# Front of a hybrid decoder block in another order, its row scale on GpSimd, and two work tiles lent to weight loads

## The chip, the cores and the metric

The kernel runs on one core of a Trainium2 chip. The metric is the device time of one execution in microseconds (us). Before the change, three runs gave 628.66, 625.45 and 625.47 us: a median of 625.47 us. The engines are named as the profile names them: PE is TensorE's matmul and PEld its weight load, DVE is VectorE, ACT is ScalarE, POOL is GpSimd, SP is SyncE, whose queue only issues DMAs here.

## What is computed

One decoder layer on 256 tokens of 1024 channels, float32 in and out:

```
h = rms_norm(x, attn_norm_w)
z = h @ w_in                      # keys, values, queries, branches, gates
y_ret = retention(...)            # 4 heads, chunks of 128
y_sc  = sb * causal_dwconv(sc * sx, sc_conv_w)
y_nsa = nsa_attention(...)        # compressed + selected + window branch
merged = g_ret*(y_ret@w_ret_out) + g_sc*(y_sc@w_sc_out) + g_nsa*(y_nsa@w_nsa_out)
x = x + merged @ w_mix_out
x = x + conv_glu_ffn(rms_norm(x, ffn_norm_w), w_up, conv_w, w_down)
return rms_norm(x, final_norm_w)
```

The compressed branch of the sparse attention takes overlapping blocks of 32 keys (and values), adds a position table, and passes each block through `gelu(blk @ w1) @ w2`. With 256 tokens all four selectable key blocks of 64 are selected, so the selected branch is causal attention over all keys.

## The kernel before, in words

**Pieces.** All weights come as pieces of 128 x 2048 float32 (1 MB), in two halves of 128 x 1024. A half is loaded into a tile `raw` by SP's queue (L129), then split in two numbers whose sum is the weight: ACT casts it to the high part `whi` (L136), DVE subtracts to get the low part `wlo` (L137). A product is three matmuls (`mm3`, L163): high x high, high x low, low x high. A piece is an `Item` with `load`, `split` and `consume`. `raw` has four buffers, so two pieces; the split parts have five pairs of buffers and, in the front, a sixth (`w_m`, in the room of a later tile): three pieces. A half's `raw` buffer is free again once DVE has its `wlo`.

**The order of the pieces.** `stream` (L175) walks a list of items: in step i it emits the loads of item i+2 (`la=2`), the split of item i+1 (`ls=1`), then the matmuls of item i and what takes their result out of PSUM (its `evac`), then what `later` had put off by one item, then `pull` steps of the generator `attention`. That is program order. Every engine runs its own instructions in one order that is fixed when the program is built; the framework keeps data dependences but may place an instruction ahead of others that stand before it in the program. `tc.keep_in_program_order` forbids it for one instruction. The result shows in the trace: the copies of the position table (L349), written long after the first value pieces, ran on ACT at 13.67 and 15.00 us.

**PSUM.** Eight banks: three in turn with the tag `mm`, five with the tag `aux`. A feature-major piece (`f_consume`, L193: keys, queries, short-convolution pieces) takes one `mm` bank; a token-major pair of pieces (`t_pair`, L210: the gates) takes two and keeps them over both pieces. A bank is free again when its evac is done.

**The front** (the first list of items): five `vv` items (values and branch gates, on x that is not yet normalized, `xw`), then `kc` and `vc` (compressed keys and values, also on `xw`, scaled by the row scale on the way out, L338), then `ks` and `kw` (selected and window keys) and everything else on the normalized `hT`. The order is: vv, kc, vc, ks, kw, gate 0, w1 0, query 0, gate 1, w1 1, gate 2, w1 2, gate 3, w1 3; and in a second list, which also pulls the attention: query 1, x0, x1, x4, b0, x2, x3, ... (x and b are the short convolution's pieces, `scx` and `sbp`).

**The row scale.** ACT squares x (L278), POOL adds the squares up (L279, L281), PE sums over partitions, DVE and POOL make `rs0` (L285, L286), DVE and PE spread it over partitions, and DVE copies it to `rstd` (L295). `head_rest` with all this stands behind the fourth vv item. `head_h` (L306) then makes `hT`: eight DVE multiplications of x by norm weight and `rstd` (L308), four ACT casts (L311), four DVE subtractions (L312). Its first half stands ahead of kc's matmuls, its second ahead of vc's. x is in the tile with the tag `ysch`, the squares in the tile with the tag `yscl`; both rooms are taken later by the short convolution's result.

**The evacs of the front.** `cmp_raw_evac` (L331) scales kc or vc into `dd` and copies it, shifted by a token, to the other 64 partitions by a DMA on ACT's queue; one item later `cmp_blocks` (L344) clears `bb` on POOL, puts the position table in (L349, L350) and splits `dd` into it (ACT L355, DVE L356). `w1_consume` multiplies `bb` with the w1 pieces. `key_evac` (L359) takes ks or kw to `kdh` and `kdl` by four ACT copies (L370) and four DVE subtractions (L371) in turn, then copies each half to the other partitions with DMAs on POOL's queue (L374). `q_evac` does the same for queries without a DMA.

**The attention** (`attention`, L648) gives 36 steps, pulled between the 23 items of the second list: scores, softmax on DVE and ACT, transposes, products with the values.

Of the kernel before, what the change touches and what calls it, by code (L numbers as in the profile page):

```python
# [63 lines left out]
def kernel(  # L64
# [55 lines left out]

    class Item:
# [4 lines left out]
        def load(self):  # L126
            for ap, n in self.srcs:
                r = wpool.tile([128, 1024], F32, tag="raw", name="raw", bufs=RAWB)
                nc.sync.dma_start(r[:, :n], ap)  # L129
                self.raw.append(r)  # L130

# [43 lines left out]
    def stream(items, gen=None, la=2, ls=1):  # L175
        n = len(items)
        for i in range(-la, n):
            if 0 <= i + la < n and not items[i + la].raw:
                items[i + la].load()
            if 0 <= i + ls < n and not items[i + ls].parts:  # L180
                items[i + ls].split()
            if i < 0:
                continue
            due = pending[:]
            pending.clear()
            items[i].consume(items[i].parts)
# [76 lines left out]
    def attw(k):  # L263
        return attn_w[:, k : k + 1]
# [34 lines left out]
    def head_rstd():  # L299
        ps = bank("aux")  # L300
        for t in range(2):
            mm(ps[:, t : t + 1], sq[:, 0, t * 128 : (t + 1) * 128], ones[:, 0:1], True, True)
        row_rstd(ps[:, 0:2], rs0)
        spread(rs0, sq[:, 1, :], rstd)

    def head_h(half):  # L306
        for k in range(4 * half, 4 * half + 4):
            V.scalar_tensor_tensor(xT_s[:, k, :], xT_s[:, k, :], attw(k), rstd, op0=OP.mult, op1=OP.mult)  # L308
            if k % 2 == 1:
                c = slice(k - 1, k + 1)  # L310
                A.copy(hT[0][:, c, :], xT_s[:, c, :])  # L311
                V.tensor_sub(hT[1][:, c, :], xT_s[:, c, :], f32(hT[0][:, c, :]))  # L312
# [18 lines left out]
    def cmp_raw_evac(kv):  # L331
        def evac(ps):
            p4 = ps.rearrange("p (b t) -> p b t", b=2)
            d = cp.tile([128, 4, S], F32, tag="dd", name="dd", bufs=2)
            dv = d.rearrange("p (b two) t -> p b two t", two=2)
            for par in range(2):
                r = slice(par * 64, par * 64 + 64)
                V.tensor_tensor(dv[0:64, :, par, :], p4[r], rstd[r].unsqueeze(1).to_broadcast([64, 2, S]), op=OP.mult)  # L338
            nc.scalar.dma_start(d[64:128, :, 0 : S - 1], d[0:64, :, 1:S])
            later(lambda: cmp_blocks(kv, d))  # L340

        return evac

    def cmp_blocks(kv, d):  # L344
# [4 lines left out]
        A.copy(bb[:, :, 0, 0, 15], pos)  # L349
        V.tensor_sub(bb[:, :, 1, 0, 15], pos, f32(bb[:, :, 0, 0, 15]))  # L350
        d5 = d.rearrange("p g (c l two) -> p l g c two", two=2, l=8)
        for i in range(2):
            src = d5[:, :, :, i : i + 15, 0]
            hi, lo = (bb[:, 8 * i : 8 * i + 8, x, :, 0:15] for x in range(2))
            A.copy(hi, src)  # L355
            V.tensor_sub(lo, src, f32(hi))  # L356
        blk[kv] = bb.rearrange("p l s g c -> p l (s g c)")

    def key_evac(name):  # L359
        def evac(ps):  # L360
            p4 = ps.rearrange("p (b t) -> p b t", b=2)
            for par in range(2):
                r = slice(par * 64, par * 64 + 64)
                o = slice(64 - par * 64, 128 - par * 64)
                kv4 = [k.rearrange("p (b two) t -> p b two t", two=2) for k in kd]
                for t in range(2):
                    c = KCOL[(name, t)]
                    src = p4[r, :, t * 128 : (t + 1) * 128]
                    dst = [k[r, :, par, c : c + 128] for k in kv4]
                    A.copy(dst[0], src)  # L370
                    V.tensor_sub(dst[1], src, f32(dst[0]))  # L371
# [109 lines left out]
    def vv_items():  # L481
        st = {}

        def go(ks, off):
            def run(parts):
# [3 lines left out]
                for k in ks:  # L489
                    hi, lo = parts[k - off]  # L490
                    for t in range(2):
# [9 lines left out]
                        )  # L501
                if ks[-1] == 7:
# [266 lines left out]
    def proj(n, **kw):  # L769
# [41 lines left out]
    stream(items)  # L811
# [9 lines left out]
    p_sc, g_nsa = proj("o_sc"), gate("o_nsa")
    made = {"x": scx, "b": sbp, "q": nqp, "s": lambda j: p_sc[j], "n": lambda j: g_nsa[j]}
    for n, e in enumerate(plan):
        items.append(made[e[0]](int(e[1])))
        items[-1].pull = (36 * (n + 1)) // len(plan) - 36 * n // len(plan)
    stream(items, att)
# [443 lines left out]
```

## Time and profile before

| | |
|---|---|
| median of three runs | 625.47 us |
| the profiled execution, its own time | 626.15 us |
| span of its profile | 624.3 us |
| busy: PE, DVE, ACT, POOL | 603.4, 477.6, 387.1, 21.2 us |
| matmuls | 3948 |
| granted TensorE clock, mean | 0.994 |
| moved by DMA | 111.82 MB |

A profile page holds one execution. Times are in us, "mean ns" in nanoseconds. The table of windows gives, for a stretch of the span, each engine's busy time with its instructions (xN), the granted TensorE clock (PEclk, 1.00 is full speed), the busy share of the DMA engines and the GB/s moved. In the timeline each row has start, duration, engine, line, operation, tile written and tiles read, and at its end, in brackets, the idle time of the engine before it and what ended it. A matmul's duration in the timeline is longer than the distance to the next one, since they are pipelined; the distance is what counts. In the table of waits a row has the waiting engine, what it waited for, the total, the times and the longest.

### The profile page before, as it was taken

The numbers are of one execution on the slowest core, as the hardware profiler recorded it, in microseconds if no ns is written. First come the engines' busy times: TensorE is split into PE (matmuls) and PEld (weight loads), VectorE is DVE, ScalarE is ACT, GpSimd is POOL, SyncE is SP. The second block draws the span as 40 slices with busy tenths as digits, with TensorE's granted clock in tenths as the row PEclk, the third lists the DMA queues.
The fourth block names the chain that finished last, engine by engine and source line by source line (L and its number), as shares of the span: only waits on it lengthen the run. The fifth ranks groups of instructions, "written<-read, shape, count | busy, mean of one in ns | idle before, by whom it ended". The sixth has DMA issues, their size and how long they took to land.

```text
span 624.3 us, 10611 instructions
## 1 busy us (share of the span) xinstructions
PE 603.4 (97%) x3948; PEld 548.2 (88%) x3948; DVE 477.6 (76%) x935; ACT 387.1 (62%) x752; POOL 21.2 (3%) x32
## 2 busy tenths in 40 slices
PE   8986999999999999999999999999999999999994
PEld 8975989999999888898888888888999999999993
DVE  6897568998989887679657977568898777777754
ACT  7665667798988887644554565446756555555532
POOL 5102000000000000000000100000000000000001
PEclk9999999999999999999999999999999999999998
DMA  7759876444354344465655477675347755566401
GB/s 257 246 174 254 236 248 221 140 162 139 108 164 136 122 147 136 136 219 171 215 193 165 132 252 247 202 265 174 109 153 254 234 178 181 186 201 202 138 1 67
DMA packets 32995, 111.82 MB, mean 179 GB/s; under 512 B 3632, under 2 KB 5552, under 8 KB 32816
## 3 DMA queue, kind: packets, MB, share of 16 engines
q1 hardware_dynamic: 30240, 106.00, 52.3%
q10 hardware_dynamic: 1552, 4.09, 2.1%
q0 software_dynamic: 1152, 1.05, 1.2%
q8 instruction: 31, 0.51, 0.3%
q14 instruction: 20, 0.16, 0.1%
HBM read 108.51 MB, written 1.05 MB: 175 GB/s over the span
## 4 chain that ended last, share of the span: by engine, by line
PE 76%; DVE 7%; ACT 7%; DMA 6%; issue 2%; POOL 1%; SPq 0%; POOLq 0%; ACTq 0%; DVEq 0%
PE ps_mm L161 56%; PE ps_aux L161 17%; DMA raw<-in_wp_dram 5%; DVE wlo L137 3%; ACT whi L136 2%; PE ps_aux L598 1%; ACT P L575 1%; DMA xT_s<-in_xT_dram 1%; DVE qs L533 0%; POOL sq L281 0%; PE ps_aux L627 0%; DVE hTl L312 0%; DVE dd L338 0%; DVE xT_s L308 0%; ACT low L641 0%
## 5 line engine op out<-in xcount | busy, mean ns | idle before, releaser
L137 DVE TENSOR_TENSOR wlo<-raw,whi 128x1024 fp32r<-128x1024 f32 (+1 forms) x197 | 237.7, 1210 | 85.8 <-ACT whi L136 84.1
L136 ACT CAST whi<-raw 128x1024 fp32r<-128x1024 f32 (+1 forms) x197 | 203.0, 1035 | 132.3 <-PE ps_mm L161 82.2
L161 PE MATMUL ps_mm<-hTh,whi 128*128 128x256 f32 x352 | 99.4, 282 | 6.2 <-DVE kdl L371 5.2
L161 PE MATMUL ps_mm<-h,whi 128*128 128x256 f32 x576 | 102.2, 281 | 0.0
L161 PE MATMUL ps_mm<-hTh,wlo 128*128 128x256 f32 x352 | 99.0, 281 | 0.5 <-DVE wlo L137 0.5
L161 PE MATMUL ps_mm<-hTl,whi 128*128 128x256 f32 x352 | 98.8, 281 | 0.6 <-DVE hTl L312 0.6
L161 PEld LDWEIGHTS ps_mm<-h,whi 128*128 128x128 f32 x576 | 88.5, 188 | 0.7
L161 PE MATMUL ps_mm<-h,wlo 128*128 128x256 f32 x288 | 80.9, 281 | 0.0
L161 PEld LDWEIGHTS ps_mm<-hTh,whi 128*128 128x128 f32 x352 | 67.1, 191 | 6.9 <-issue 5.3
L161 PEld LDWEIGHTS ps_mm<-hTl,whi 128*128 128x128 f32 x352 | 67.1, 191 | 1.3 <-DVE hTl L312 1.0
L161 PEld LDWEIGHTS ps_mm<-hTh,wlo 128*128 128x128 f32 x352 | 67.0, 190 | 0.9 <-DVE wlo L137 0.9
L161 PE MATMUL ps_mm<-whi,hTh 128*128 128x512 f32 x152 | 59.7, 393 | 0.0
L161 PE MATMUL ps_mm<-whi,hTl 128*128 128x512 f32 x152 | 59.3, 390 | 0.0
L161 PE MATMUL ps_mm<-wlo,hTh 128*128 128x512 f32 x152 | 59.3, 390 | 0.0
L161 PEld LDWEIGHTS ps_mm<-h,wlo 128*128 128x128 f32 x288 | 55.3, 192 | 0.0
L575 ACT ACTIVATE P<-P,st 128x16 f32<-128x16 f32 (+2 forms) x96 | 37.9, 397 | 0.8 <-DVE st L570 0.7
L161 PE MATMUL ps_aux<-whi,acth 128*128 128x512 f32 x88 | 34.2, 389 | 0.0
L161 PE MATMUL ps_aux<-wlo,acth 128*128 128x512 f32 x88 | 34.2, 389 | 0.0
L161 PE MATMUL ps_aux<-whi,actl 128*128 128x512 f32 x88 | 34.2, 389 | 0.0
L161 PEld LDWEIGHTS ps_mm<-whi,hTl 128*128 128x128 f32 x152 | 28.5, 188 | 6.1
L161 PEld LDWEIGHTS ps_mm<-whi,hTh 128*128 128x128 f32 x152 | 28.6, 188 | 5.6
L161 PEld LDWEIGHTS ps_mm<-wlo,hTh 128*128 128x128 f32 x152 | 28.6, 188 | 5.5
(250 smaller groups left out, 1141.2 us busy)
## 6 DMA issues: line engine op xcount, KB each, us to landing
raw<-in_wp_dram SPq DMA_DIRECT2D x194, 512.0 KB, 4.4
raw<-in_wv_dram SPq DMA_DIRECT2D x8, 280.0 KB, 3.9
x2b<-in_xt_dram ACTq DMA_DIRECT2D x1, 1024.0 KB, 4.7
xT_s<-in_xT_dram SPq DMA_DIRECT2D x3, 256.0 KB, 6.0
rct<-in_rc_dram ACTq DMA_DIRECT2D x1, 768.0 KB, 5.9
kdh<-kdh POOLq DMA_DIRECT2D x4, 128.0 KB, 6.6
kdl<-kdl POOLq DMA_DIRECT2D x4, 128.0 KB, 7.1
finb<-in_fin_dram ACTq DMA_DIRECT2D x1, 512.0 KB, 3.5
```

The source lines that it names most:

```text
L136: A.copy(hi[:, :n], r[:, :n])
L137: V.tensor_sub(lo[:, :n], r[:, :n], f32(hi[:, :n]))
L161: return T.matmul(o, l, r, start=start, stop=stop, skip_group_check=True)
L575: A.activation(pp, pp, AF.Exp, bias=st[:, r : r + 1], scale=-1.0, accum_out=sm[:, r : r + 1])
L598: T.transpose(pt[:, dst : dst + 128], u["P"][(t, pr)][:, c : c + 128], ident)
```

## The change

The front's list is reordered, with x0, x1 and query 1 moved into it from the second list, and the position of three pieces of other work is moved with it. The core of the diff:

```
+    def raw_ring(n):
+        return [wpool.tile([128, 1024], F32, tag="raw", name="raw", bufs=RAWB) for _ in range(n)]
+    raws, loads = [raw_ring, raw_ring], [0]
...
         def load(self):
-            for ap, n in self.srcs:
-                r = wpool.tile([128, 1024], F32, tag="raw", name="raw", bufs=RAWB)
+            for (ap, n), r in zip(self.srcs, raws[loads[0] % len(raws)](len(self.srcs))):
                 nc.sync.dma_start(r[:, :n], ap)
                 self.raw.append(r)
+            loads[0] += 1
...
+    def wait_pieces(n, f):
+        later(f if n == 1 else lambda: wait_pieces(n - 1, f))
...
-    def stream(items, gen=None, la=2, ls=1):
+    def stream(items, gen=None, nxt=(), la=2, ls=1):
         n = len(items)
+        items = items + list(nxt)
         for i in range(-la, n):
-            if 0 <= i + la < n and not items[i + la].raw:
-                items[i + la].load()
-            if 0 <= i + ls < n and not items[i + ls].parts:
+            if 0 <= i + la < len(items):
+                for it in items[max(i, 0) : i + la + 1]:
+                    if not it.raw:
+                        it.load()
+            if 0 <= i + ls < len(items) and not items[i + ls].parts:
                 items[i + ls].split()
...
     def head_rstd():
         ps = bank("aux")
         for t in range(2):
-            mm(ps[:, t : t + 1], sq[:, 0, t * 128 : (t + 1) * 128], ones[:, 0:1], True, True)
+            tc.keep_in_program_order(
+                mm(ps[:, t : t + 1], sq[:, 0, t * 128 : (t + 1) * 128], ones[:, 0:1], True, True)
+            )
         row_rstd(ps[:, 0:2], rs0)
+    def head_spread():
         spread(rs0, sq[:, 1, :], rstd)
     def head_h(half):
-        for k in range(4 * half, 4 * half + 4):
-            V.scalar_tensor_tensor(xT_s[:, k, :], xT_s[:, k, :], attw(k), rstd, op0=OP.mult, op1=OP.mult)
-            if k % 2 == 1:
-                c = slice(k - 1, k + 1)
-                A.copy(hT[0][:, c, :], xT_s[:, c, :])
-                V.tensor_sub(hT[1][:, c, :], xT_s[:, c, :], f32(hT[0][:, c, :]))
+        for c in range(2 * half, 2 * half + 2):
+            x2k = xT_s[:, 2 * c : 2 * c + 2, :]
+            G.tensor_tensor(x2k, x2k, rstd.unsqueeze(1).to_broadcast([128, 2, S]), op=OP.mult)
+            for k in (2 * c, 2 * c + 1):
+                A.activation(hT[0][:, k, :], xT_s[:, k, :], AF.Copy, scale=attw(k))
+                V.scalar_tensor_tensor(
+                    hT[1][:, k, :], xT_s[:, k, :], attw(k), f32(hT[0][:, k, :]), op0=OP.mult, op1=OP.subtract
+                )
...
-            later(lambda: cmp_blocks(kv, d))
+            wait_pieces(4 if kv else 2, lambda: cmp_blocks(kv, d))
...
                 for k in ks:                      # vv items
...
+                        if (k, t) == (6, 0):
+                            head_rest()
+                        if (k, t) == (7, 0):
+                            head_spread()
...
         g_sc[0],
+        g_sc[1],
         piece("w1", 0, w1_consume(0, 0)),
+        g_sc[2],
+        g_sc[3],
+        piece("w1", 1, w1_consume(0, 1)),
         nqp(0),
-        g_sc[1],
-        piece("w1", 1, w1_consume(0, 1)),
-        g_sc[2],
+        nqp(1),
         piece("w1", 2, w1_consume(1, 0)),
-        g_sc[3],
+        scx(0),
+        scx(1),
         piece("w1", 3, w1_consume(1, 1)),
     ]
-    then(vv[3], head_rest)
...
-    stream(items)
+    plan = "x4 b0 x2 x3 q2 x6 b1 x5 x7 b2 q3 b3 s0 s1 n0 n1 s2 s3 n2 n3".split()
...
+    cut = 9
+    stream(items[:cut], nxt=items[cut:])
+    def wide(tag):
+        def get(n):
+            z = yp.tile([128, 2, 1024], F32, tag=tag, name="raw_w")
+            return [z[:, 0, :], z[:, 1, :]]
+        return get
+    raws += [wide("ysch"), wide("yscl")]
+    stream(items[cut:-3], nxt=items[-3:], la=4)
+    del raws[2:]
+    stream(items[-3:], nxt=late[:2])
...
-    plan = "q1 x0 x1 x4 b0 x2 x3 q2 x6 b1 x5 x7 b2 q3 b3 s0 s1 n0 n1 s2 s3 n2 n3".split()
...
-    stream(items, att)
+    stream(late, att)
```

In words:

- The order after kw is gate 0, gate 1, w1 0, gate 2, gate 3, w1 1, query 0, query 1, w1 2, x0, x1, w1 3. The list that pulls the attention has 20 items instead of 23; it still pulls 36 steps.
- From gate 0 on the loads run four items ahead (`la=4`) and, besides the four `raw` buffers, go in turn into the rooms of x (`ysch`) and of the squares (`yscl`), one piece each: w1 0 into `yscl`, w1 1 into `ysch`, query 0 into `yscl`, x0 into `ysch`, x1 into `yscl`. For the last three items and the second list there are the four `raw` buffers again. Each list also loads and splits the first items of the next one ahead (`nxt`).
- The partition sums of the row scale are pinned behind the matmuls of the value chunk k=6 for the first 128 tokens, and the spread behind those of k=7.
- `head_h`: four POOL multiplications of 128 x 512 by `rstd`, eight ACT activations with the norm weight as scale, eight DVE operations that give the low part.
- `cmp_blocks` of the keys runs two pieces after kc's evac (behind ks), that of the values four pieces after vc's (behind gate 1). Its copies of the position table and its splits are pinned in program order on ACT and DVE ("tables pinned").
- `key_evac` and `q_evac` emit their ACT copies first and their DVE operations after them, instead of in turn.

More of the change, by code (lines that the diff above doesn't have):

```diff
@@ L348, in cmp_blocks @@
         pos = cvt[:, CV_POS + 16 * kv : CV_POS + 16 * kv + 16]
-        A.copy(bb[:, :, 0, 0, 15], pos)
-        V.tensor_sub(bb[:, :, 1, 0, 15], pos, f32(bb[:, :, 0, 0, 15]))
+        tc.keep_in_program_order(A.copy(bb[:, :, 0, 0, 15], pos))
+        tc.keep_in_program_order(V.tensor_sub(bb[:, :, 1, 0, 15], pos, f32(bb[:, :, 0, 0, 15])))
         d5 = d.rearrange("p g (c l two) -> p l g c two", two=2, l=8)
@@ L354, in cmp_blocks @@
             hi, lo = (bb[:, 8 * i : 8 * i + 8, x, :, 0:15] for x in range(2))
-            A.copy(hi, src)
-            V.tensor_sub(lo, src, f32(hi))
+            tc.keep_in_program_order(A.copy(hi, src))
+            tc.keep_in_program_order(V.tensor_sub(lo, src, f32(hi)))
         blk[kv] = bb.rearrange("p l s g c -> p l (s g c)")
@@ L361, in evac @@
             p4 = ps.rearrange("p (b t) -> p b t", b=2)
+            kv4 = [k.rearrange("p (b two) t -> p b two t", two=2) for k in kd]
+            job = []
+            for par in range(2):
+                r = slice(par * 64, par * 64 + 64)
+                for t in range(2):
+                    c = KCOL[(name, t)]
+                    job.append((p4[r, :, t * 128 : (t + 1) * 128], [k[r, :, par, c : c + 128] for k in kv4]))
+            for src, dst in job:
+                A.copy(dst[0], src)
+            for src, dst in job:
+                V.tensor_sub(dst[1], src, f32(dst[0]))
             for par in range(2):
@@ L364, in evac @@
                 o = slice(64 - par * 64, 128 - par * 64)
[L365 to L371, printed above, removed]
                 c = min(KCOL[(name, t)] for t in range(2))
@@ L528, in evac @@
             qs = at.tile([128, 2, 2, S], F32R, tag="qs", name="qs", bufs=2)
+            rows = [slice(0, 64), slice(64, 128)]
             for par in range(2):
-                r = slice(par * 64, par * 64 + 64)
-                o = slice((1 - par) * 64, (1 - par) * 64 + 64)
+                r = rows[par]
                 A.mul(qs[r, par], p4[r], 0.125)
+            for par in range(2):
+                r, o = rows[par], rows[1 - par]
                 V.scalar_tensor_tensor(qs[o, par], p4[r], 0.125, f32(qs[r, par]), op0=OP.mult, op1=OP.subtract)
@@ L810 @@
     V.tensor_scalar(rethalf, x_s[:, KB : 2 * KB], 0.5, None, op0=OP.mult)
-    stream(items)
+    att = attention()
+    late = []
+    plan = "x4 b0 x2 x3 q2 x6 b1 x5 x7 b2 q3 b3 s0 s1 n0 n1 s2 s3 n2 n3".split()
+    p_sc, g_nsa = proj("o_sc"), gate("o_nsa")
+    made = {"x": scx, "b": sbp, "q": nqp, "s": lambda j: p_sc[j], "n": lambda j: g_nsa[j]}
+    for n, e in enumerate(plan):
+        late.append(made[e[0]](int(e[1])))
+        late[-1].pull = (36 * (n + 1)) // len(plan) - 36 * n // len(plan)
+    cut = 9
[9 more added lines that the diff above has]
+    stream(items[-3:], nxt=late[:2])
     ysc = [yp.tile([128, KB, S], F32R, tag=n, name=n) for n in ("ysch", "yscl")]
@@ L816 @@
     aw = aw_es.enter_context(pool("aw"))
-    att = attention()
-    items = []
-    plan = "q1 x0 x1 x4 b0 x2 x3 q2 x6 b1 x5 x7 b2 q3 b3 s0 s1 n0 n1 s2 s3 n2 n3".split()
[L821 to L825, printed above, removed]
-    stream(items, att)
+    stream(late, att)
     for _ in att:
```

## The prediction

> **What bounds the kernel now.** The page comes first, then the stretches, the waits and the timeline of the front.
>
> ```profile
> span 624.3 us, 10611 instructions
> PE 603.4 (97%) x3948; PEld 548.2 (88%) x3948; DVE 477.6 (76%) x935; ACT 387.1 (62%) x752; POOL 21.2 (3%) x32
> ```
>
> PE bounds the kernel, and the change removes no matmul, so only time in which PE stands or runs slow can be won. The chain of waits says where pieces run undisturbed and where they don't:
>
> ```profile
> 89.74 2.51 PE ps_aux L161 x20
> 97.95 1.04 PE ps_aux L161 x4
> 111.86 2.27 PE ps_aux L161 x20
> 182.55 5.48 PE ps_mm L161 x48
> ```
> ```profile
> 22.22 0.28 PE L161 MATMUL ps_mm<-ynsah,whi 128*128 128x256 f32 x1
> ```
>
> A piece alone takes 5.48 us (48 matmuls, 0.114 each), a w1 piece 16/20 of 2.51, so 2.0. From kc's first matmul (22.22) to x1's last (111.86) pass 89.6 us. In them lie twelve pieces (kc, vc, ks, kw, four gates, q0, q1, x0, x1), 65.8, and four w1 pieces, 8.0. Three attention steps and the compressed branch's small matmuls between them (the 1.04 at 97.95 is one such group) I put at 3.6. That is 77.4, so about 12.2 us are lost here. The rest of the kernel holds no such loss that this change touches. Where the 12.2 lie:
>
> ```profile
> 30.00:40.00 10.00, 8.11 (x62) 7.31 (x61) 9.54 (x15) 6.60 (x9) 0.00 (x0) 1.00 0.57 190
> 40.00:50.00 10.00, 9.73 (x76) 9.01 (x75) 9.56 (x12) 5.93 (x9) 1.93 (x3) 1.00 0.68 192
> 50.00:60.00 10.00, 5.78 (x33) 4.87 (x31) 6.97 (x9) 5.56 (x8) 1.98 (x4) 1.00 1.25 251
> 60.00:70.00 10.00, 9.06 (x57) 8.76 (x58) 4.44 (x5) 3.76 (x4) 0.92 (x2) 0.83 1.11 276
> ```
> ```profile
> PE ps_mm L161 <- DVE kdl L371: 5.2, 1, 5.2
> PE ps_mm L161 <- ACT hTh L311: 1.0, 1, 1.0
> PE ps_aux L161 <- POOL sq L281: 0.5, 1, 0.5
> PE ps_aux L161 <- DVE sq L293: 0.3, 1, 0.3
> ```
>
> Two places. First, 30 to 40: DVE is 95% busy and DMA moves only 190 GB/s, against 251 and 276 later: loads wait for `raw`, `raw` waits for DVE. In that stretch ks waits for `hT`:
>
> ```profile
> 35.49 0.28 PE L161 MATMUL ps_mm<-hTh,whi 128*128 128x256 f32 x1
> 36.80 0.38 PE L161 MATMUL ps_mm<-hTh,whi 128*128 128x256 f32 x1 [1.04 <-ACT hTh L311]
> ```
>
> Here 1.2 are lost beyond a normal 0.11; with the shorter breaks on `hTl` and a late `wlo` I estimate 3.0 over ks and kw. Second, 55 to 64: w1 0 ends and query 0 can't start.
>
> ```profile
> 55.49 0.28 PE L161 MATMUL ps_aux<-wlo,bb 128*128 128x256 f32 x1
> 60.94 0.55 PE L161 MATMUL ps_mm<-hTh,whi 128*128 128x256 f32 x1 [5.16 <-DVE kdl L371]
> 61.28 0.41 PE L161 MATMUL ps_mm<-hTl,whi 128*128 128x256 f32 x1
> 61.50 0.41 PE L161 MATMUL ps_mm<-hTh,wlo 128*128 128x256 f32 x1
> ```
> ```profile
> 56.02 1.04 ACT L136 CAST whi<-raw 128x1024 fp32r<-128x1024 f32 x1 [1.69 <-DMA raw<-in_wp_dram]
> 58.03 1.04 ACT L136 CAST whi<-raw 128x1024 fp32r<-128x1024 f32 x1 [0.58 <-DMA raw<-in_wp_dram]
> 59.10 0.37 ACT L370 CAST kdh<-ps_mm 64x256 fp32r<-64x256 f32 x1
> ```
> ```profile
> 60.36 0.43 DVE L371 TENSOR_TENSOR kdl<-ps_mm,kdh 64x256 fp32r<-64x256 f32 x1
> ```
>
> The named releaser is kw's PSUM bank: its evac's copies stand in ACT's queue behind casts that wait for DMA. But query 0's own weights were cast only at 56.02 and 58.03, so without the bank it would still have started about 57 to 58. The loss is 5.3 in the gap. Behind it the matmuls stand 0.22 apart (61.28 to 61.50): the granted clock of 60 to 70 is 0.83, so 3.4 us at half speed, another 1.7. Together 7.0.
>
> **The change part by part.**
>
> Row scale pinned into the last value piece. Removed: PE's 0.5 and 0.3 above, with their ramps 0.9. Added: PE stands in its queue if the sums aren't there; POOL's last sum ended at 16.45 + 1.11 = 17.56, and the pinned place comes at about 17.8. But kc can't start before its first `wlo`:
>
> ```profile
> 20.73 1.22 DVE L137 TENSOR_TENSOR wlo<-raw,whi 128x1024 fp32r<-128x1024 f32 x1
> ```
>
> It ended at 21.95; between nothing won and 0.9 I take 0.6.
>
> Row multiplication on POOL. From
>
> ```profile
> L308 DVE SCALAR_TENSOR_TENSOR xT_s<-xT_s,rstd 128x256 f32<-128x256 f32 x8 | 3.4, 478 | 0.0
> L312 DVE TENSOR_TENSOR hTl<-xT_s,hTh 128x512 fp32r<-128x512 f32 x4 | 2.7, 681 | 1.2 <-ACT hTh L311 1.2
> L356 DVE TENSOR_TENSOR bb<-dd,bb 128x480 fp32r<-128x480 f32 x4 | 4.0, 1023 | 0.1
> ```
>
> DVE loses 6.1 us of work and gets eight two-input operations of L308's shape, 3.6 with their gaps: 2.5 saved. ACT gets eight activations for four casts, about 1.3 more, in a stretch where it is 66% busy. POOL gets four of twice the size of its sums. The price is that POOL and DVE slow each other:
>
> ```profile
> 15.64 0.73 POOL L279 TENSOR_TENSOR sq<-sq 128x256 f32<-128x256 f32 x1
> 16.45 1.11 POOL L281 TENSOR_TENSOR sq<-sq 128x256 f32<-128x256 f32 x1
> ```
> ```profile
> 13.43 0.73 DVE L137 TENSOR_TENSOR wlo<-raw,whi 128x560 fp32r<-128x560 f32 x1
> 15.81 2.34 DVE L137 TENSOR_TENSOR wlo<-raw,whi 128x560 fp32r<-128x560 f32 x2
> ```
>
> Two DVE operations of 0.73 took 2.34, so 0.88 more, beside 1.84 of POOL: 0.48 per us. Four POOL operations of 1.46 (twice 0.73), stretched by 1.11/0.73 to at most 8.9 in all, cost DVE 2.8 to 4.2, so DVE's work is no smaller. What is won is the order: POOL doesn't stand behind the weight splits, as the second half of L308 did, so x is scaled by about 30 instead of 36.9, the end of
>
> ```profile
> 35.23 1.67 DVE L308 SCALAR_TENSOR_TENSOR xT_s<-xT_s,rstd 128x256 f32<-128x256 f32 x4
> ```
> DVE also loses the key blocks' 2.0 between vc and ks. ks then waits 0 to 2.6; I take 1.0: of the 3.0, 2.0 won.
>
> [...]
>
> New order, loads four ahead. Where query 0 stood behind w1 0, there is now gate 2, with gate 1 ahead of w1 0, so 5.48 us more of PE work cover the loads; kw's bank is wanted 5 us later, and its four ACT copies no longer alternate with DVE. Each load into `raw` takes
>
> ```profile
> DMA to landing us min/median/max: 4.2/6.5/8.9
> ```
>
> in the stretch 30 to 62, so a cycle through four halves (6.5, then 1.04 cast and 1.2 subtraction) gives a half per 2.2 us at best: nearly PE's whole pace, and less than DMA can. With w1 0 and w1 1 in other rooms this limit goes. On SP's queue the order stays; only a load whose buffer isn't free holds those behind it, and the squares' room is free from the spread (20), x's from `hT` (36), both before their first load. The key copies on POOL's queue (1.05 MB, at POOL's issue) now fall to about 39 to 50, behind POOL's multiplications, which have ended.
>
> Kept in order: the blocks `bb`. Those of the keys (2.0 on DVE, as much on ACT) move between ks's evac and gate 0's split, and gate 0 is late by 0.7. Those of the values stand behind gate 1's evac. Queued behind them on ACT is gate 2's split, for which PE waits: 2.0 of blocks, 1.04 cast and 1.2 subtraction against w1 0's 2.0 on PE give up to 2.2; if the split is placed ahead, 0. I take 1.2. Of the 7.0, 5.1 won. Deeper loads take away the small waits of the w1 and query stretch: 0.4.
>
> Attention over 20 items. Nothing is removed, but each item carries 1.8 steps instead of 1.57.
>
> ```profile
> 130.00:150.00 20.00, 19.85 (x170) 19.52 (x169) 17.66 (x54) 16.71 (x49) 0.00 (x0) 1.00 0.40 133
> 150.00:170.00 20.00, 19.24 (x159) 18.57 (x158) 18.61 (x60) 18.47 (x56) 0.00 (x0) 1.00 0.42 133
> ```
>
> At 88% of DVE PE loses 0.15 in 20 us, at 93% 0.76. The twelve dense items (x, b, q) last about 88 us; if they all went from the first to the second, 2.7 more. Lower end 0; I take 1.2. (x0, x1 and q1 themselves cost the same PE time in the front; their evacs, 1.4 of DVE each, lie beside it where DVE isn't full.)
>
> Sum: 0.6 + 2.0 + 5.1 + 0.4 - 1.2 = 6.9 won. The profiled execution took 626.15 (span 624.3 and 1.85 around it); 0.7 above the median of 625.47. Taken off the median: **618.5 us**.
>
> **The rivals.**
>
> *The gap moves.* Gate 2 waits for its load or its split as query 0 did, with the clock halved behind. For: the GB/s of 50 to 70 are the highest of the front, so DMA itself was near its limit; casts of later pieces can again be queued ahead of evacs. Against: 190 GB/s earlier leaves room to load ahead. Price: 7.0 instead of 1.9, so 623.6.
>
> *The row scale gets stuck.* kc's split now stands ahead of the row scale in the program. If DVE's fixed order has both of kc's subtractions before L285, the scale waits for kc's second half, whose load came late:
>
> ```profile
> 21.15 1.05 ACT L136 CAST whi<-raw 128x1024 fp32r<-128x1024 f32 x1 [1.52 <-DMA raw<-in_wp_dram]
> ```
>
> ```profile
> 18.25 0.16 DVE L285 TENSOR_SCALAR rs<-ps_aux 128x2 f32<-128x2 f32 x1
> ...
> 19.24 0.48 DVE L293 TENSOR_SCALAR sq<-ident,rs 128x128 f32<-128x128 f32 x2 [0.83 <-POOL rs L286]
> ```
>
> Cast to 22.2, `wlo` to 23.4, then 1.5 to the spread (18.25 to 19.72 here): PE, pinned, waits till 24.9 instead of going on at about 19.8. Part is given back since ks then waits no longer: 3.5 more, 622.0. That the framework orders things otherwise than the diff says is this rival too.
>
> [...]
>
> *Slower: the attention runs short of ACT and DVE.* A step is a chain PE, DVE, ACT, DVE, ACT, PE; if two steps no longer fit beside a dense item, each of the twelve loses the wait that is left. From 0.7 us each on (8.1 over 12) the gain is used up; at 1.3 each the time is 618.5 + 15.6 - 1.2 = 632.9. For: 92% of ACT in 150 to 170. Against: an item's casts and evac, some 3 us of ACT, don't grow; with 2.8 items in that row 10 of its 18.47 do, by 15%, to 19.9 in all, while PE's 20 become 20.7; and the row itself lost only 0.76.
>
> **How the numbers follow.** About 0.5%, 3.1 us, is what a measurement of this kernel can tell from no change. Forecast 0.66 (own range 614 to 622, nearly all faster), the moved gap 0.12 (mostly within 0.5%), the stuck scale 0.08 (half and half), POOL shutting DVE out 0.08 (faster), slower 0.06. So faster 0.66 x 0.97 + 0.12 x 0.2 + 0.08 x 0.5 + 0.08 = 0.78, slower 0.06, the same 0.16. The range goes from 613.5 (nothing left of the waits that I let stand, 1.9, 1.0 and 1.2, and 0.9 of small ones won besides) to 623.7, which takes in the moved gap and the two milder rivals.
>
> **What would show it.** Right: no PE wait over 2 us between 20 and 100, and the granted clock 1.00 there; x scaled on POOL by 30 and ks's wait on `hT` under 1.5; x1 ended about 100 before any attention step; DMA over 220 GB/s in 30 to 50; PE's busy time in the attention stretch down by about a per cent. Wrong: a PE wait of 4 or more behind w1 0 or at the spread; a DVE pace of over 1.8 per 1024-column subtraction while POOL multiplies; losses of a us or more per item among x, b and q.

## The result, and the profile after

The changed kernel takes 615.68 us (median of four runs, 615.43 to 616.11); the kernel before, run beside it, 625.81 (four runs, 625.45 to 628.66). The ratio is 0.983, 95% interval 0.9805 to 0.9856: faster by 10.1 us, where 6.9 were forecast. The profiled execution took 615.45 with a span of 613.6, against 626.15 and 624.3. All numbers below compare these two profiles unless another kernel is named.

The page of the kernel after, first lines:

```profile
span 613.6 us, 10606 instructions
PE 600.8 (98%) x3948; PEld 547.0 (89%) x3948; DVE 476.9 (78%) x931; ACT 387.7 (63%) x756; POOL 28.7 (5%) x36
```

The matmuls are the same 3948, and PE's busy time is 2.6 lower, 1.7 of it because the 3.4 us at half clock are gone. POOL took over the row multiplication, 7.5 us more of it; DVE's total hardly fell (477.6 to 476.9), as its instructions became longer. The windows of the stretches that the prediction showed (PE, PEld, DVE, ACT, POOL, granted clock, DMA share, GB/s):

```profile
30.00:40.00 10.00, 9.12 (x75) 8.72 (x74) 9.88 (x17) 4.26 (x7) 0.00 (x0) 1.00 0.89 246
40.00:50.00 10.00, 10.00 (x76) 9.43 (x75) 8.63 (x12) 6.47 (x10) 2.52 (x4) 1.00 1.02 333
50.00:60.00 10.00, 10.00 (x53) 8.60 (x52) 8.55 (x11) 8.54 (x14) 2.32 (x4) 1.00 1.25 281
60.00:70.00 10.00, 10.00 (x45) 8.26 (x44) 8.40 (x9) 7.91 (x9) 0.00 (x0) 1.00 1.12 334
```

From 40 to 70 PE is never idle and the clock is 1.00 throughout; before, PE was busy for only 5.78 of the 10 us from 50 to 60, and the clock was 0.83 in the ten behind. DMA moves 246 to 334 GB/s where it moved 190 to 276. PE's waits in the first 112 us:

```profile
PE ps_mm L167 <- DVE wlo L143: 1.4, 2, 0.9
PE ps_aux L167 <- DVE mhalf L267: 1.1, 1, 1.1
PE ps_aux L167 <- ACT whi L142: 0.7, 1, 0.7
PE ps_aux L167 <- POOL sq L294: 0.2, 1, 0.2
```

Query 0's 5.2 is gone, and `hT` is waited for no more. Behind 20 us only the first row is left. The two waits of the first row, in the PE timeline:

```profile
28.72 0.38 PE L167 MATMUL ps_mm<-ynsah,wlo 128*128 128x256 f32 x1 [0.57 <-DVE wlo L143]
...
35.49 0.38 PE L167 MATMUL ps_mm<-hTh,wlo 128*128 128x256 f32 x1 [0.88 <-DVE wlo L143]
```

One is in vc (28.72) and new, one at the start of ks (35.49). In the same timeline x1 ends at 98.15 and the front at 100.08. What POOL did meanwhile, and DVE beside it:

```profile
22.81 7.01 POOL L326 TENSOR_TENSOR xT_s<-xT_s,rstd 128x512 f32<-128x512 f32 x4 [2.52 <-DVE rstd L308]
```
```profile
20.78 1.22 DVE L143 TENSOR_TENSOR wlo<-raw,whi 128x1024 fp32r<-128x1024 f32 x1
...
22.64 1.21 DVE L143 TENSOR_TENSOR wlo<-raw,whi 128x1024 fp32r<-128x1024 f32 x1
23.78 1.32 DVE L533 TENSOR_SCALAR sg<-sg 128x48 f32<-128x48 f32 x1
25.01 0.86 DVE L502 SCALAR_TENSOR_TENSOR vz<-ps_aux,rs,vz 128x256 fp32r<-128x256 f32 x2
25.80 0.54 DVE L537 TENSOR_SCALAR sg<-sg,cmt 128x16 f32<-128x16 f32 x1
...
26.35 2.32 DVE L143 TENSOR_TENSOR wlo<-raw,whi 128x1024 fp32r<-128x1024 f32 x1
28.59 2.31 DVE L143 TENSOR_TENSOR w_m<-raw,w_m 128x1024 fp32r<-128x1024 f32 x1
```

POOL ends at 29.82, so x is scaled 7 us earlier than before. Two subtractions take 2.3 instead of 1.2, and two tiny operations on the branch gates (`sg`) 1.32 and 0.54.

**Where the 10.7 us of span came from**, cut at the starts of the same matmuls in both traces. Query 1, x0 and x1 (3 x 5.48 = 16.44) moved from the second list to the front and are taken off on both sides:

| stretch | before | after | won | forecast |
|---|---|---|---|---|
| to kc's first matmul | 22.22 | 22.10 | 0.1 | 0.6 |
| kc and vc | 11.36 | 12.11 | -0.75 | 0 |
| ks and kw | 14.47 | 12.51 | 2.0 | 2.0 |
| gate 0 to w1 3 (the rest of the front) | 44.01 | 53.36 - 16.44 | 7.1 | 5.1 + 0.4 |
| list with the attention | 173.99 - 16.44 | 155.69 | 1.9 | -1.2 |
| behind it | 358.25 | 357.83 | 0.4 | 0 |

The first and the last row lie within what two executions differ by: the same kernel run again (a_again below) has 22.38 and 358.26 there. Its four rows between, 12.08, 12.51, 53.35 - 16.44 and 155.72, repeat to 0.03.

### The profile page after: what moved, and what is told of

It is laid out like the page before. It is cut to its first block, busy times and chain, and to the rows that moved or that the text cites. A ratio compares the mean times of both kernels' runs of the same rounds, so it can differ in the third digit from the quotient of the medians.

```text
span 613.6 us, 10606 instructions
## 1 busy us (share of the span) xinstructions
PE 600.8 (98%) x3948; PEld 547.0 (89%) x3948; DVE 476.9 (78%) x931; ACT 387.7 (63%) x756; POOL 28.7 (5%) x36
## 4 chain that ended last, share of the span: by engine, by line
PE 88%; ACT 4%; DVE 4%; POOL 1%; issue 1%; DMA 1%; SPq 0%; POOLq 0%; ACTq 0%
PE ps_mm L167 66%; PE ps_aux L167 19%; PE ps_aux L627 1%; DVE wlo L143 1%; ACT whi L142 1%; DMA xT_s<-in_xT_dram 1%; ACT P L604 1%; POOL sq L294 0%; PE ps_aux L656 0%; ACT ph L630 0%; POOL sq L292 0%; DVE hnb L1049 0%; PE ps_mm L782 0%; POOL bb L366 0%; PE ps_aux L976 0%
## 5 line engine op out<-in xcount | busy, mean ns | idle before, releaser
L143 DVE TENSOR_TENSOR wlo<-raw,whi 128x1024 fp32r<-128x1024 f32 (+1 forms) x187 | 226.4, 1215 | 77.8 <-ACT whi L142 76.2
L142 ACT CAST whi<-raw 128x1024 fp32r<-128x1024 f32 (+1 forms) x187 | 192.4, 1034 | 116.5 <-PE ps_mm L167 75.5
L167 PE MATMUL ps_mm<-hTh,wlo 128*128 128x256 f32 x328 | 91.5, 279 | 0.9 <-DVE wlo L143 0.9
L167 PE MATMUL ps_mm<-hTh,whi 128*128 128x256 f32 x328 | 91.9, 280 | 0.0
L167 PE MATMUL ps_mm<-hTl,whi 128*128 128x256 f32 x328 | 91.6, 279 | 0.0
L167 PEld LDWEIGHTS ps_mm<-hTh,wlo 128*128 128x128 f32 x328 | 61.8, 189 | 1.3 <-DVE wlo L143 1.1
L167 PEld LDWEIGHTS ps_mm<-hTl,whi 128*128 128x128 f32 x328 | 61.8, 188 | 0.5 <-DVE hTl L329 0.2
L167 PEld LDWEIGHTS ps_mm<-hTh,whi 128*128 128x128 f32 x328 | 61.7, 188 | 0.5 <-issue 0.4
```

The source lines that it names most:

```text
L142: A.copy(hi[:, :n], r[:, :n])
L143: V.tensor_sub(lo[:, :n], r[:, :n], f32(hi[:, :n]))
L167: return T.matmul(o, l, r, start=start, stop=stop, skip_group_check=True)
```

## The experiments

The theory going in was the prediction's: order and loads close query 0's gap, POOL's multiplication shortens ks, and the attention pays a little. The rivals put the gap down to one PSUM bank alone, or the gain to the rooms, or to the pinned blocks. Twelve kernels ran, on three chips, each beside the kernel before (medians 626.99, 627.07 and 627.38); "won" is one minus the ratio, times 626. The intervals reach 1 to 2 us to either side, so two rows that lie closer than that are told apart only where the text names their runs.

| kernel | median | ratio, 95% interval | won |
|---|---|---|---|
| before, query 0 in an aux bank (b_q0_aux) | 626.1 | 0.9996, 0.9972 to 1.0019 | 0 |
| before, the new order alone (b_order) | 619.57 | 0.9886, 0.9853 to 0.9918 | 7.1 |
| after without rooms (a_no_rooms) | 617.17 | 0.9852, 0.9823 to 0.9882 | 9.3 |
| after, old order (a_order_old) | 621.8 | 0.9915, 0.989 to 0.9939 | 5.3 |
| after, row multiplication on DVE (a_h_dve) | 616.62 | 0.9849, 0.9825 to 0.9872 | 9.5 |
| after, blocks early and not pinned (a_no_pins) | 620.47 | 0.9891, 0.9874 to 0.9908 | 6.8 |
| after, q1, x0, x1 back in the second list (a_late23) | 618.5 | 0.9862, 0.9845 to 0.988 | 8.6 |
| after, DVE work put off (a_dve_later) | 617.66 | 0.985, 0.9821 to 0.9879 | 9.4 |
| after unchanged (a_again) | 616.19 | 0.9822, 0.9799 to 0.9845 | 11.1 |
| after, DVE work put off, gates first (a_gates_first) | 615.22 | 0.9812, 0.9786 to 0.9839 | 11.8 |
| after without rooms, multiplication on DVE (a_order_pins) | 617.11 | 0.9844, 0.982 to 0.9867 | 9.8 |
| after, only three small operations put off (a_sg_later) | 614.83 | 0.9801, 0.9777 to 0.9825 | 12.5 |

### Was it only the PSUM bank? (b_q0_aux)

```
-            ps = bank("mm")
+            ps = bank(tag)
...
-        return piece("nq", g, f_consume(hT, q_evac(g)), side=SIDE, **kw)
+        return piece("nq", g, f_consume(hT, q_evac(g), tag="mm" if g else "aux"), side=SIDE, **kw)
```

> The kernel before, with query 0's matmuls in one of the five aux banks, so that it no longer waits for kw's evac. If the 5.2 us that PE waited there belong to the PSUM bank (rival), the gap closes, the clock stays at 1.00 and the time falls by 5 to 7 us to about 619. If they belong to the loads (theory: four halves in flight, each 4.2 to 8.9 us on its way), query 0 starts at about 57.3 behind its first cast (56.02 + 1.04), stops again for its second half (cast to 59.1, low part to 60.3), and the time falls by 1 to 2.5 us, to 623 to 624.5.

The gap is gone and the time is the same: 626.1. In this kernel's PE timeline query 0 starts right behind w1 0:

```profile
56.45 0.30 PE L161 MATMUL ps_aux<-hTh,whi 128*128 128x256 f32 x1
```

The time is lost again 15 us later. Its windows and its waits from 50 to 100:

```profile
70.00:80.00 10.00, 8.70 (x43) 6.62 (x44) 7.44 (x8) 7.39 (x11) 0.00 (x0) 1.00 0.67 236
80.00:90.00 10.00, 7.57 (x40) 6.22 (x39) 5.92 (x7) 6.22 (x10) 0.00 (x0) 0.97 0.78 262
```
```profile
PE ps_aux L437 <- DVE cq_lo L428: 2.4, 1, 2.4
PE ps_aux L161 <- ACT cq_lo L415: 1.0, 1, 1.0
```

Both waits are for `cq_lo`, the work tile of the compressed branch, the first behind gate 2, the second behind gate 3. The operations that make the second stand on ACT and DVE behind splits of weights whose loads were late:

```profile
82.34 1.05 ACT L136 CAST whi<-raw 128x1024 fp32r<-128x1024 f32 x1 [1.64 <-DMA raw<-in_wp_dram]
83.29 0.37 ACT L424 ACTIVATE cq_lo<-ps_aux 64x256 f32<-64x256 f32 x1
```
```profile
85.16 1.22 DVE L137 TENSOR_TENSOR wlo<-raw,whi 128x1024 fp32r<-128x1024 f32 x1 [0.32 <-ACT whi L136]
86.42 0.41 DVE L426 TENSOR_TENSOR cq_lo<-cq_lo,ps_aux 64x256 f32<-64x256 f32 x1
```

So the bank was what PE stood for at 55, and by this trace late loads are what the stretch lacked: PE starts query 0 4.5 us earlier (60.94 before), then stands 1.0 and 2.4 behind gates 2 and 3, and the granted clock is 0.97 in 80 to 90 (above). Neither side's number holds as it was written. The 5.2 of that wait's row is no price of the bank.

### The order alone, and the change without it (b_order, a_order_old)

The first puts the new order into the kernel before (and `plan` without q1, x0, x1), the second the old order into the kernel after:

```
         g_sc[0],
+        g_sc[1],
         piece("w1", 0, w1_consume(0, 0)),
-        nqp(0),
-        g_sc[1],
+        g_sc[2],
+        g_sc[3],
         piece("w1", 1, w1_consume(0, 1)),
+        nqp(0),
+        nqp(1),
...
+        scx(0),
+        scx(1),
```

> The kernel before with the new order of the pieces alone (gate 0, gate 1, w1 0, gate 2, gate 3, w1 1, query 0, query 1, w1 2, x0, x1, w1 3, then 20 items with the attention): no rooms, no POOL multiplication, nothing pinned. Theory (order and rooms share the gain): the gap of 5.2 behind w1 0 shrinks to 1 to 3, since gate 1's 5.5 us cover loads, but loads still go at 2.2 to 2.6 us a half; time 619 to 622. Rival (the order does it all): no gap over 1 us behind kw, time about 618. Rival (rooms do it all): the gap stays, 624 or more.

> The kernel after with the old order of the pieces (and 23 items with the attention), rooms, POOL and pins kept. Theory (order and rooms share the gain): w1 0's load lies in a room and comes early, but query 0 still stands only 2 us of PE work behind gate 0 and w1 0; a gap of 1 to 4 us at query 0 or behind, time 617 to 620. Rival (the rooms do it all): no wait over 1 us, 615 to 616.5. Rival (order does it all): the gap of 5 with the halved clock, 622 or more.

The order alone wins 7.1 of some 11: no wait above 1.8 is left from 20 to 100, with two `raw` pieces and the old evacs. The waits of b_order, the two largest:

```profile
PE ps_aux L161 <- ACT cq_lo L415: 1.8, 1, 1.8
PE ps_mm L161 <- ACT hTh L311: 1.0, 1, 1.0
```

`hT` is still waited for, as it should be. The time is in the theory's range (619 to 622). The profile is of the longest of its four runs (621.05; two others took 618.24 and 618.27). Cut as in the table above, it wins 3.2 from gate 0 to w1 3 (40.82) and 1.65 in the list with the attention (155.90). So in this run the order alone gives less than half of the 7.1 that the kernel after wins from gate 0 to w1 3.

With the old order in the kernel after, the old wait on kw's evac is back at half its size, and half clock with it. Windows and waits of a_order_old:

```profile
50.00:60.00 10.00, 7.43 (x44) 6.77 (x43) 8.87 (x12) 8.86 (x13) 2.32 (x4) 0.90 1.25 292
60.00:70.00 10.00, 10.00 (x59) 9.04 (x59) 7.63 (x9) 6.23 (x8) 0.00 (x0) 0.93 1.07 308
```
```profile
PE ps_mm L167 <- DVE kdl L391: 2.6, 1, 2.6
```

Its span is 620.0, 6.4 above the kernel after: 2.6 of wait, 1.7 of clock (0.10 and 0.07 of ten us each lost), 1.7 in its attention list of 23 items, and the rest in kc to kw. The gap is as the theory had it (1 to 4), the time 1.8 above its range. All other parts together, without the order, win 3.0 from gate 0 to w1 3 (41.05).

### The rooms (a_no_rooms)

```
-    raws += [wide("ysch"), wide("yscl")]
-    stream(items[cut:-3], nxt=items[-3:], la=4)
+    stream(items[cut:-3], nxt=items[-3:])
```

> The kernel after without the two lent rooms and with loads two items ahead, all else kept. Theory: loads are again limited by four halves in flight; DMA falls from about 333 GB/s in 40 to 70 to some 200 to 260, PE waits 2 to 5 us at gate 1, w1 0 or gate 2, time 618 to 621. Rival (the order alone is enough): DMA slower, but no PE wait over 1 us, time 615 to 616.5.

617.17, or 1.0 to 1.5 above the two medians of the kernel after (615.68 and 616.19, on other runs of the kernel before): by the intervals that can't be told from nothing. The theory's 618 to 621 missed, and so did the rival's time (615 to 616.5), but the rival's sign came: no PE wait over 0.9 from 20 to 100. The profile is of its shortest run, with a_again's span, 614.3. DMA falls to 254 GB/s in 60 to 70 (334 with the rooms), and PE doesn't notice:

```profile
60.00:70.00 10.00, 10.00 (x45) 8.26 (x45) 8.46 (x9) 8.34 (x11) 0.00 (x0) 1.00 0.82 254
```

### The row multiplication back on DVE (a_h_dve)

```
-            G.tensor_tensor(x2k, x2k, rstd.unsqueeze(1).to_broadcast([128, 2, S]), op=OP.mult)
+            V.tensor_tensor(x2k, x2k, rstd.unsqueeze(1).to_broadcast([128, 2, S]), op=OP.mult)
```

> The kernel after with the four multiplications of x by the row scale on DVE instead of POOL. In the profile after, DVE's 1024-column subtractions took 2.3 us instead of 1.2 while POOL multiplied, and DVE was delayed by about 3.6 in all. Theory (POOL costs DVE about what it saves): the subtractions are back at 1.2, DVE has 2.8 more of its own, the wait of 0.74 in vc goes, ks waits 1 to 2 more on hT; time within 1 us of after, 615 to 617. Rival (POOL is a main part of the gain): 618 or more.

Its DVE timeline shows the subtraction at its old pace, so it was POOL that stretched it:

```profile
24.89 1.23 DVE L143 TENSOR_TENSOR wlo<-raw,whi 128x1024 fp32r<-128x1024 f32 x1
```

and its waits show what POOL had bought:

```profile
PE ps_mm L167 <- DVE wlo L143: 1.6, 1, 1.6
PE ps_mm L167 <- ACT hTh L328: 0.9, 1, 0.9
```

By the medians it is 616.62 against 615.68 and 616.19, no difference that can be told. Its five runs lie in two groups, 615.93 to 616.62 and 619.38 to 619.84. The two in the upper group had a mean clock of 0.992, the other three 0.995 to 0.997. The profile is of the longest and shows half clock behind the waits:

```profile
35.00:40.00 5.00, 3.40 (x17) 2.91 (x18) 4.97 (x9) 2.75 (x5) 0.00 (x0) 0.76 0.80 219
40.00:45.00 5.00, 5.00 (x28) 5.00 (x27) 4.94 (x6) 2.09 (x2) 0.00 (x0) 0.55 0.81 251
```

### The blocks early and not pinned (a_no_pins)

```
-            wait_pieces(4 if kv else 2, lambda: cmp_blocks(kv, d))
+            later(lambda: cmp_blocks(kv, d))
...
-            tc.keep_in_program_order(A.copy(hi, src))
-            tc.keep_in_program_order(V.tensor_sub(lo, src, f32(hi)))
+            A.copy(hi, src)
+            V.tensor_sub(lo, src, f32(hi))
```

> The kernel after with the blocks bb made one piece behind their key or value piece and free to be placed, as before the change. Theory: ACT's copies of the key blocks now stand ahead of gate 0's second cast and wait for the dd copy, which takes 7.9 us to land beside the loads; PE waits 0 to 2 us at gate 0; time 615.5 to 617.5. Rival (the pins are a main part): a wait of 3 us or more, 618.5 or more.

Between 4 and 5 us are lost: 620.47. In its ACT timeline a block's cast waits 2.12 for its shift DMA, with a second one after it, and the next splits stand behind both:

```profile
40.02 1.05 ACT L374 CAST bb<-dd 128x480 fp32r<-128x480 f32 x1 [2.12 <-DMA dd<-dd]
...
41.90 1.04 ACT L142 CAST whi<-raw 128x1024 fp32r<-128x1024 f32 x1
42.84 1.04 ACT L142 CAST w_m<-raw 128x1024 fp32r<-128x1024 f32 x1
```
```profile
PE ps_mm L167 <- DVE wlo L143: 4.9, 2, 3.2
```
```profile
40.00:45.00 5.00, 1.81 (x13) 1.62 (x13) 3.90 (x4) 3.86 (x4) 0.00 (x0) 0.84 0.93 326
45.00:50.00 5.00, 5.00 (x25) 5.00 (x25) 4.70 (x8) 3.42 (x7) 1.52 (x3) 0.50 0.88 240
```

PE waits 1.7 in vc and 3.2 in kw, then runs at half clock from about 43 to 50. The rival's signs came (3 us or more, 618.5 or more), the theory's time did not. The prediction had the later, pinned blocks as 2.0 less DVE work ahead of ks and as a cost (0.7 at gate 0, 1.2 at gate 2); what the early ones would cost in kw it did not have. Which of the two edits does it, the later place or the pin, was not tried apart.

### Three pieces back in the attention's list (a_late23)

```
-        nqp(1),
         piece("w1", 2, w1_consume(1, 0)),
-        scx(0),
-        scx(1),
...
+    plan = "q1 x0 x1 x4 b0 x2 x3 q2 x6 b1 x5 x7 b2 q3 b3 s0 s1 n0 n1 s2 s3 n2 n3".split()
```

> The kernel after with query 1, x0 and x1 back in the list that pulls the attention (23 items, 1.57 steps each instead of 1.8). The prediction's term: with 20 items PE loses 1.2 more there; then 614.5. Theory now: the share of steps costs nothing, and three pieces of PE work less stand beside the w1 loads, so PE waits 0 to 3 us in the front at the last w1 pieces; time 615.5 to 618.5.

It is slower than the kernel after by some 2.5 us (618.5; spans 616.1 and 613.6), inside the theory's range but not for its reason: no PE wait over 0.8 stands in the front behind 20 us, and the loss is in the attention. The sums over 110 to 250 us, of the kernel after, of a_late23 and of the kernel before:

```profile
sum 140.00, PE 139.43 PEld 127.18 DVE 123.57 ACT 122.39 POOL 0.00; mean PE 19.92 PEld 18.17 DVE 17.65 ACT 17.48 POOL 0.00
```
```profile
sum 140.00, PE 137.93 PEld 126.39 DVE 120.38 ACT 119.62 POOL 0.00; mean PE 19.70 PEld 18.06 DVE 17.20 ACT 17.09 POOL 0.00
```
```profile
sum 140.00, PE 138.20 PEld 128.24 DVE 121.53 ACT 118.45 POOL 0.00; mean PE 19.74 PEld 18.32 DVE 17.36 ACT 16.92 POOL 0.00
```

PE stands 0.6 with the list of 20 items and about 2 with 23, although DVE and ACT are busier in the first. In the list of 23 PE's largest wait is for the attention's own softmax (1.0 and 1.2 on ACT's `pc`), in the list of 20 there is none for `pc`. The other kernels say the same. Cut as in the table of stretches, with 16.44 taken off where the list has 23 items, it takes 155.69 to 155.90 in all ten traces with 20 items (155.90 is b_order's), and 157.43 to 159.19 in the four with 23 (159.19 is a_late23's, which has 0.6 of the compressed branch's matmuls in it besides). The list as the cause is shown; why more steps per item wait less is not.

### Less DVE work beside POOL (a_dve_later, a_gates_first, a_again, a_sg_later, a_order_pins)

The first puts off kc's scaling into `dd` by a piece and the three `sg` operations by five pieces; the second adds an order with the four gates ahead of w1 0; the third is the kernel after again, for the same chip; the fourth puts off the `sg` operations alone:

```
-                        V.tensor_scalar(sg[:, t, :], sg[:, t, :], 1.0, 0.5, op0=OP.add, op1=OP.mult)
...
-                    cg = sg[:, 0, :].rearrange("p (h b) -> p h b", b=3)[:, :, 0:1]
-                    V.tensor_scalar(cg, cg, cmt[:, CM_ANY : CM_ANY + 1], None, op0=OP.mult)
+                    wait_pieces(5, sg_rest)
```

> The kernel after with less on DVE ahead of the splits of vc and ks: kc's scaling into dd one piece later (its blocks one piece later too), and the three small operations on the branch gates five pieces later. Theory: the last waits in the front, 0.74 in vc and 1.05 in ks, are DVE's order alone; they shrink by 1 to 2 us in all; time 614 to 615. Rival (they hang on DVE's whole load between 20 and 40): the wait moves to kw or gate 0; time within 0.4 of after.

> kc's scaling and the gate operations later on DVE, as in the run before, and all four gate pieces ahead of w1 0, so that the key blocks have 11 us more (order: gates 0 to 3, w1 0, query 0, w1 1, query 1, w1 2, x0, x1, w1 3). Theory: the wait of 1.5 us at w1 0 goes and none takes its place; no wait over 0.6 us between 20 and 100 us, the clock stays at 1.00 in every run; time 1.5 to 2.5 us under after, 613 to 614.5. Rival (DVE's load of 20 to 45 comes due elsewhere): a wait of a us or more at kw, gate 0 or gate 1, time within 0.7 of after.

> The kernel after, unchanged, beside the next three on one chip. If its waits (0.7 and 1.1 us in vc and ks) never bring the granted clock down, its times lie within 1 us of each other, near 615.7; if they sometimes do, some lie 3.4 us higher, as the two groups of times of the last kernels did.

> The kernel after with only the three small operations on the branch gates five pieces later. Theory: they cost DVE 2 us beside POOL (0.19 us alone, 1.32 beside it) just ahead of vc's split; the wait of 0.74 in vc goes, that in ks stays; time 0.5 to 1 under after. Rival: the subtractions just meet POOL earlier, nothing gained.

a_again's four runs lie within 0.2 of each other, with a mean clock of 0.995 to 0.997: in none of them did the waits bring the clock down. a_dve_later takes vc's and ks's waits away and gets a new one, the blocks for w1 0:

```profile
PE ps_aux L167 <- DVE bb L381: 1.4, 1, 1.4
```

Its median, 617.66, says little: its six runs lie in two groups, 615.05 to 616.24 with a mean clock of 0.995 to 0.997, and 619.07 to 620.98 with 0.992 or 0.993. The profile is of the lower group, which is about level with the kernel after, where 614 to 615 had been expected.

With the gates ahead of w1 0 that wait is gone, as expected, and none over 0.5 is left behind 20 us. The time is 615.22, one below a_again's 616.19 where 1.5 to 2.5 had been expected; four of its five runs are below a_again's, one above. a_sg_later does as much with less: 614.83, its four runs (614.45 to 615.32) all below the four of a_again (616.11 to 616.24) on the same chip; the intervals of the two ratios overlap. Its DVE timeline and its only wait from 20 to 100:

```profile
24.94 1.53 DVE L143 TENSOR_TENSOR wlo<-raw,whi 128x1024 fp32r<-128x1024 f32 x1
27.09 1.61 DVE L143 TENSOR_TENSOR w_m<-raw,w_m 128x1024 fp32r<-128x1024 f32 x1 [0.62 <-ACT w_m L142]
```
```profile
PE ps_mm L167 <- DVE wlo L143: 0.8, 1, 0.8
```

The subtractions start earlier and meet POOL's instructions at another point, take 1.5 and 1.6 instead of 2.3, and vc's wait is gone; POOL's four take 8.1 instead of 7.0, and the first two of the four operations for `hT`'s low part, at 29.02, take 2.55, where all four took 1.66 in the kernel after. So part of the rival (the subtractions just meet POOL elsewhere) is true too. It has the lowest median of all kernels here.

a_order_pins takes the rooms and POOL's multiplication out together, by the two diffs shown above:

> The kernel after without the lent rooms, with loads two ahead and with the row multiplication on DVE: of the change the order, the pinned and later blocks, the pinned row sums and the evacs in groups are left. Theory (these carry the gain; rooms and POOL are worth 0.5 to 1 us each): 616.5 to 618.5, with a wait of 2 to 3 us at ks, and in some runs 3.4 us more by the clock. Rival (rooms or POOL are needed together): 620 or more in all runs.

617.11, in the theory's range: it keeps 9.8 of some 11, so the order and the pinned later blocks, with the smaller edits beside them, carry the gain. Rooms and POOL together are worth about 1: all five runs (616.53 to 618.75) are above a_again's on the same chip. From gate 0 to w1 3 it wins the same 7.1 as the kernel after (36.91), and so does a_no_pins (36.92). So what b_order's trace lacks there needs neither the rooms and POOL's multiplication nor the pinned blocks; it may be the smaller edits that all these kernels share. (The smaller ones, the pinned row scale, ACT's scaled casts and the key evac's order, were not tried alone.)

## Why the prediction was right, point by point

The direction, the place and the two largest terms were right; the time came out 2.8 below 618.5 and inside the range. Of the 3.8 of span won beyond the forecast, 3.1 come from the attention, whose term had the wrong sign, and 1.6 from the new order; 0.5 and 0.75 at the start, in kc and vc went the other way. By its own steps:

*Row scale pinned: mechanism right, size not settled.* 0.6 was taken between 0 and 0.9; 0.1 came in this pair of traces. PE's wait there did go from 0.8 to 0.2, but kc's first `wlo` ends at 22.00 and kc starts at 22.10, which was the reason given for the lower end. In the other traces of kernels with the pin kc starts between 21.26 and 22.54, so one pair can't tell 0.1 from 0.6.

*POOL's multiplication: right in sum, partly by luck, with one sign misjudged.* ks and kw won 2.0 as forecast, x is scaled at 29.8, and the remaining wait at ks is 0.9. But two pieces alone take 10.96, so these stretches had lost 3.5 before, not 3.0, and lose 1.55 after, not 1.0: two equal errors. DVE's delay is (1.32 - 0.19) + (0.54 - 0.23) + (2.32 - 1.22) + (2.31 - 1.22) = 3.6, inside 2.8 to 4.2; the undisturbed 0.19 and 0.23 are from a_h_dve's trace. But it sits on single instructions: the pace of two subtractions, 2.3, is over the 1.8 that the prediction had named as a sign of being wrong. That sign was set as if the delay were spread evenly. It did cost something: the subtraction that ends at 28.67 makes vc wait 0.57, part of the -0.75 that the prediction had at nothing (without POOL, in a_h_dve's trace, kc and vc take 11.35). And by a_h_dve the whole part is worth no more than about 1, probably since DVE, without POOL beside it, gets its own work done sooner. The forecast gives POOL shutting DVE out a chance of 0.08; no run shows DVE shut out for all of POOL's time. The trace shows three single instructions with 1.1 more each, where one of POOL's four takes 1.75 on average, and 3.6 of delay in all beside POOL's 7.01. Two `vz` operations with an input in PSUM took 0.86 together beside POOL, and 0.87 in a_h_dve's trace without it.

*New order: right, and larger.* 7.1 of 7.0 and 0.4 instead of 5.1 and 0.4: from gate 0 to the end of the front PE waits for nothing, so neither the 0.7 at gate 0 nor the 1.2 at gate 2 came. That it needs the order and not the rooms is shown by a_order_old (3.0 of the 7.1 without the order) and a_no_rooms (6.9 without the rooms). That the order alone does it is not shown: b_order's trace has 3.2, and what adds the rest was not tried alone.

*How the gap was read: wrong in a step.* "Query 0's own weights were cast only at 56.02 and 58.03" took the wrong halves. Every sixth half of the front goes to `w_m`; the one at 60.76 is gate 1's second, so 58.03 is gate 1's first and query 0's are the casts at 53.01 and 56.02. ACT's timeline of the kernel before, for the whole row of them:

```profile
53.01 1.05 ACT L136 CAST whi<-raw 128x1024 fp32r<-128x1024 f32 x1 [1.38 <-DMA raw<-in_wp_dram]
53.96 0.36 ACT L370 CAST kdh<-ps_mm 64x256 fp32r<-64x256 f32 x1
56.02 1.04 ACT L136 CAST whi<-raw 128x1024 fp32r<-128x1024 f32 x1 [1.69 <-DMA raw<-in_wp_dram]
...
60.76 1.04 ACT L136 CAST w_m<-raw 128x1024 fp32r<-128x1024 f32 x1 [1.30 <-DMA raw<-in_wp_dram]
```

So the bank alone held query 0, by its evac's copies standing behind casts that waited for loads. The conclusion (the loads are the limit, the bank is no cure) came out right for another reason, as b_q0_aux shows.

*DMA's limit: too low.* 276 GB/s in 60 to 70 was taken as near DMA's limit, in the rival of the moved gap; 333 and 334 were moved after. Nor does "on SP's queue the order stays" hold: in the trace after, the two halves of the first load into a room stand next to each other in the program and are issued at 24.31 and 31.31, with two loads into `raw` between them. It cost nothing that shows.

*Attention: wrong in sign.* -1.2 was forecast, 1.9 came. The step that failed is "At 88% of DVE PE loses 0.15 in 20 us, at 93% 0.76", two rows read as a rule. After:

```profile
130.00:150.00 20.00, 19.88 (x160) 19.08 (x159) 19.04 (x66) 19.16 (x58) 0.00 (x0) 1.00 0.43 142
150.00:170.00 20.00, 19.90 (x165) 19.39 (x164) 18.75 (x63) 17.42 (x53) 0.00 (x0) 1.00 0.49 157
```

DVE is 95% busy in the first row, ACT 96%, and PE loses 0.12. The share of DVE doesn't tell what PE loses here; the forecast of one per cent less PE in the attention was wrong, and the slower rival argued from the same rows. "The rest of the kernel holds no such loss that this change touches" was wrong as well: of the 140 us from 110 to 250 PE stood 1.8 before and 0.6 after.

*Not in the forecast:* what the pinned, later blocks save in kw (a_no_pins).

## What to carry to other kernels

A wait's row names what PE stood for last, not what the stretch lacks: where loads were late, freeing the named buffer only moved the wait on here (5.2 us before, 2.4 and 1.0 in b_q0_aux), and other PE work put ahead of it (the order) shrank it (none above 1.8 in b_order). Work that waits for a DMA, put early into the queue of the engine that also splits the weights, held the next splits back here (a cast that waited 2.12 us in a_no_pins, and PE 3.2 behind it); put it late and keep it there (which of the two mattered here is open). When two engines slow each other, as POOL and DVE did here (a subtraction 2.3 us instead of 1.2, POOL's four multiplications 7.0 or 8.1), take even the smallest instructions out of the shared stretch first: three of some 0.2 us each were worth about 1 us.

## What the runs showed of the hardware

The granted clock fell to half here for stretches of about 3.4 us or twice that, after waits that were mostly shorter. From the windows above: 3.4 us in a_order_old after a wait of 2.6; (0.24 + 0.45) x 5 / 0.5 = 6.9 in a_h_dve after 1.6 and 0.9; (0.16 + 0.50) x 5 / 0.5 = 6.6 in a_no_pins after 3.2. In a_order_pins's PE timeline the matmuls stand 0.21 apart from 38.49 to 41.91, so for 3.4 us, and 0.12 behind, after waits of only 0.8 and 0.5 within 2 us. b_order's 1.8, a_order_old's own 1.7 in vc and the kernel after's 0.9 cost none, so the length of a wait alone didn't decide here. Behind these waits of 0.5 to 3.2 us, then, 1.7 more was lost (a_order_old, a_order_pins), 3.3 or 3.45 (a_no_pins, a_h_dve), or nothing. That is probably why the times of a_h_dve and a_dve_later fall into two groups some 3 us apart, with the lower mean clock in the upper one; no kernel was profiled in both of its groups. It is not the only reason why runs differ: a_late23's lie at 617.6 to 617.9 and 619.1 to 619.3 without such a difference in clock.

DMA moved 333, 281 and 334 GB/s in the three windows from 40 to 70 after, with buffers for eight halves at a time, and 274 and 254 in the first and the last of them with buffers for four (a_no_rooms).
